# Which PSUM pool a level's product of the gated linear attention takes its bank from

## The chip, the cores and the metric

The kernel runs on one core of a Trainium2 chip. A core has five engines that run side by side, each with its own queue in order: TensorE (PE, matrix products; PEld is its loading of weights), VectorE (DVE), ScalarE (ACT), GpSimd (POOL) and SyncE (SP, which here only issues transfers). PE writes its products to PSUM, which this kernel uses as eight banks of 128 x 512 float32. DVE and ACT read them from there. The metric is the device time of one execution in microseconds (us). Lower is better.

## The reference

One layer of a hybrid decoder over 16 meta tokens and 2048 real tokens of width 1024. A normalised input u goes through one wide projection. Its columns feed two branches: a Mamba-2 state space scan (SSD, 16 heads in 4 groups, chunks of 128) and a gated linear attention (GLA, 4 heads, chunks of 64 in the reference). Both are normalised, projected, weighted by sigmoid gates, summed, projected again and added to the input. The part that the change touches is the attention within a chunk:

```python
rel = gi[:, :, :, None, :] - gi[:, :, None, :, :]
rel = jnp.exp(jnp.where(causal, rel, -jnp.inf))
att = jnp.einsum('bhtk,bhsk,bhtsk->bhts', qi, ki, rel)
o_intra = jnp.einsum('bhts,bhsv->bhtv', att, vi)
```

`gi` is the running sum of the log decay, so that each pair (t, s) has a decay of its own for every one of the 128 key channels.

## The kernel before, in words

The work has two phases. The first takes the 2048 tokens in four blocks of 512. Per block it projects u for four SSD groups and then for four GLA heads (`ssd_proj`, `gla_proj`), and beside these projections it runs the scans (`ssd_scan`, `gla_scan`). The products of the projections are float32 made of three products of rounded halves (`accum`, L188 to L190). The second phase makes the gates, the two branch projections and the output projection by a product scheme of seven products in place of eight (`Stage`).

**Order.** The scans are Python generators. After each part of a projection, `step()` takes every running scan one `yield` further, the oldest first, so that a scan's few products stand on PE between long runs of projection products. In the first phase the order of PE and of SP is the one written by hand. In the second only SP's is. The rest (DVE, ACT, POOL, and PE in the second phase) is put in order by a planner at build time, which has a model of the times.

**GLA scan.** For one head and one block of 512 tokens, `gla_scan` does not form the decay of each pair. It builds the triangle of a chunk in seven levels, with blocks of 1, 2, 4, 8, 16, 32 and 64 rows. `pack` (ACT, L706) gathers the operand of a level, `level` makes two 128 x 128 products per level on PE (L712, float32, which the profile shows as two records each), then takes over the part that belongs to the level: for the first level a copy on ACT (L717), for the others a predicated copy on DVE (L720). DVE then multiplies keys and queries by the decay of that level (L725), and `pack` gathers for the next. There are 16 such scans with 7 levels, 112 in all, mostly one level per step. After the levels, `diag` (L757), the transposes of keys and of the scores (L769, L774), four chunk products `po` with the running state (L782 to L791), and transposes of the output (L801, read by L802) follow.

**PSUM.** Three pools share the eight banks: `pj` (3) for the projections, `pt` (3) for transposes and small products, `pc` (2) for the scans' products. A tile gets a bank when a bank of its pool has been read for the last time, and the first product into it waits for that. The users in the first phase are:

- `pc`: in `ssd_scan` the scores (L529), and per chunk `py` (L572, L573, read by L580 and L583) and `pst` (L575, read by L578). In `gla_scan` the four `po` (read by L787, L789 and L791), in block 0 the meta products (L524, L743), and before the change the levels.
- `pt`: in `ssd_scan` a chunk's three transposes (L548, read by L551, L553, L554 and L557) and the two output transposes (L607, read by L609). In `gla_scan` the meta keys of block 0 (L735, read by L737), `diag`, L769, L774 and L801. Elsewhere the row factors of u (L281), the small products of `dt_chain` (L400 to L418) and of `gates`. Two tiles are held for long: one of the four of the first projection of a block (`zm`, L461), and in block 0 a head's meta values (`pv5`, L634, read by L638).

Of the kernel before, what the change touches and what calls it, by code (L numbers as in the profile page):

```python
# [40 lines left out]
def trunk_kernel(ctx: ExitStack, tc: tile.TileContext, xm, xmt, w_feat, w_tok, w_zm, w_br, w_o,  # L41
# [7 lines left out]
    def mk(pool, shape, dt, tag, **kw):  # L49
        cnt[0] += 1  # L50
        return pool.tile(shape, dt, tag=tag, name=f"{tag}_{cnt[0]}", **kw)
# [72 lines left out]
    pt = ctx.enter_context(tc.tile_pool(name="pt", bufs=3, space=bass.MemoryType.PSUM))  # L124
    pc = ctx.enter_context(tc.tile_pool(name="pc", bufs=2, space=bass.MemoryType.PSUM))

    def bank(pool, tag):
        return mk(pool, [P, 512], F32, tag)
# [534 lines left out]
    def gla_scan(o, h, kq, vals, gs):  # L663
# [5 lines left out]
        def odd_even(half, start, nb, skip):  # L669
            pitch = list(kq.ap[0])  # L670
            return bass.AP(kq.tensor, kq[:, 0, start:].offset, [pitch, [2 * half, nb], [skip, 2], [1, half]])
# [31 lines left out]
        def pack(half):  # L703
            packed[0] = mk(wk, [P, 2 * P], F32, "c1", bufs=NC1)
            nb = P // half
            nc.scalar.activation(packed[0].rearrange("p (b two h) -> p b two h", two=2, h=half),  # L706
                                 odd_even(half, m0, nb, k_to_q + 2 * P + half), AF.Copy)

        def level(half):
            ps = bank(pc, "pc")  # L710
            for r in range(2):
                nc.tensor.matmul(ps[:, r * P:(r + 1) * P], packed[0][:, r * P:(r + 1) * P],  # L712
                                 odd_even(half, m0 + (r + 2) * P, P // (2 * half), k_to_q - 2 * P + half),
                                 start=True, stop=True)
            pv2 = ps[:, :256].rearrange("p (r t) -> p r t", t=P)
            if half == 1:
                nc.scalar.activation(xa, pv2, AF.Copy)  # L717
            else:
                mi = msk[:, LEVELS.index(half)].unsqueeze(1).to_broadcast([P, 2, P])
                nc.vector.copy_predicated(xa, mi, pv2)  # L720
            nb = BLK // (2 * half)
            kv = odd_even(half, m0, nb, k_to_q + half)
            at = place[half][0]
            other = bass.AP(ex.tensor, ex[:, at + 1:].offset, [list(ex.ap[0]), [2, nb], [-1, 2], [0, half]])
            nc.vector.tensor_tensor(kv, kv, other, op=ALU.mult)  # L725
            if half < P // 2:
                pack(2 * half)

        pack(1)
        yield  # L730
        level(1)
        yield
        if m0:
            ps = bank(pt, "pt")
            nc.tensor.transpose(ps[:META, :P], km, ident)  # L735
            btm = mk(wk, [P, P], F32, "bt")
            nc.scalar.activation(btm[:META], ps[:META, :P], AF.Copy)  # L737
        level(2)
        yield
        level(4)  # L740
        yield
        if m0:
            ps = bank(pc, "pc")  # L743
# [23 lines left out]
        ps = bank(pt, "pt")  # L767
# [4 lines left out]
        ps = bank(pt, "pt")  # L772
# [25 lines left out]
        for j in range(2):  # L798
            ps = bank(pt, "pt")
# [238 lines left out]
    for st in stages:  # L1038
        begins.append(len(order))
        for n in range(0, st.npairs, 2):  # L1040
            ps = PS if (st, n) != (stages[-1], st.npairs - 2) else PS[:5] + (4, 3)
# [176 lines left out]
```

## Time and profile before

| what | value |
|---|---|
| time, median of 3 runs | 2353.59 us (2347.39 to 2354.49) |
| the profiled execution's own time | 2356.76 us |
| its span in the trace | 2355.0 us |
| PE busy | 2261.0 us, 96% of the span |
| PEld busy | 1963.7 us, 83% |
| DVE busy | 1450.1 us, 62% |
| ACT busy | 1143.9 us, 49% |
| POOL busy | 678.5 us, 29% |
| granted TensorE clock, mean | 0.986 |

The span runs from the first to the last instruction, and the own time is that of the whole execution. Busy is the time in which an engine ran an instruction. An engine's idle time is put down to the instruction that released it. The ends of products are modelled in the trace, so that short idle times of PE are less sure than long ones. The first phase ends at about 1565 us of the span.

### The profile page before, as it was taken

The page shows a single profiled execution, that of the slowest core. Times are in us where ns is not written, and L with a number is a line of the kernel's source. Part 1 is how long each engine was busy: PE and PEld are TensorE (multiplying, and loading weights), DVE is VectorE, ACT ScalarE, POOL GpSimd, SP SyncE. Part 2 cuts the span into 40 slices and gives each one's busy share as a digit, 9 for nine tenths or more (in the row PEclk, how much of TensorE's full clock was granted, in tenths as well). Part 3 has the DMA queues.
Part 4 walks back from the last instruction along what each step waited for, and adds up shares of the span by engine and source line. Part 5 has one row for each costly group of instructions (what it writes and reads, how often), then busy time and mean ns, then how long its engine had stood idle before and what let it go on. Part 6 is the DMA issues. An engine that isn't in the chain of part 4 may idle for free. (4 is left out here: it accounts for less than half of the span.)

```text
span 2355.0 us, 35946 instructions
## 1 busy us (share of the span) xinstructions
PE 2261.0 (96%) x12673; PEld 1963.7 (83%) x12673; DVE 1450.1 (62%) x2547; ACT 1143.9 (49%) x2582; POOL 678.5 (29%) x681
## 2 busy tenths in 40 slices
PE   7999999999899999999999999979999999999998
PEld 6889888898788988888888888868888888888876
DVE  5666655466554466655447654455578964779776
ACT  5656544365533265633346443354545454554443
POOL 4344333122211122221112200027433355323331
PEclk9999999999999999999999999989999999999999
DMA  8666765668676676766577644457677876688743
GB/s 305 228 207 225 254 226 200 215 206 252 213 242 201 210 223 216 255 213 222 173 226 245 209 143 165 134 168 249 209 246 264 292 235 214 225 284 272 257 155 123
DMA packets 301540, 518.01 MB, mean 220 GB/s; under 512 B 27696, under 2 KB 143664, under 8 KB 301360
## 3 DMA queue, kind: packets, MB, share of 16 engines
q1 hardware_dynamic: 200400, 402.84, 52.6%
q10 hardware_dynamic: 100960, 112.88, 13.8%
q8 instruction: 99, 1.62, 0.3%
q14 instruction: 81, 0.66, 0.1%
HBM read 368.42 MB, written 147.19 MB: 219 GB/s over the span
## 5 line engine op out<-in xcount | busy, mean ns | idle before, releaser
L188 PE MATMUL pj<-u,whl 128*128 128x512 f32 (+1 forms) x1184 | 448.7, 379 | 14.4 <-ACT acc L481 7.7
L190 PE MATMUL pj<-u,whl 128*128 128x512 f32 (+1 forms) x1184 | 432.9, 366 | 1.4 <-DVE dw L391 0.8
L189 PE MATMUL pj<-u,whl 128*128 128x512 f32 (+1 forms) x1184 | 432.2, 365 | 0.0
L188 PE MATMUL pj<-whl,u 128*128 128x256 f32 (+1 forms) x992 | 291.5, 294 | 2.2 <-ACT u L306 1.5
L190 PE MATMUL pj<-whl,u 128*128 128x256 f32 (+1 forms) x992 | 283.9, 286 | 1.4 <-DVE u L308 1.4
L189 PE MATMUL pj<-whl,u 128*128 128x256 f32 (+1 forms) x992 | 283.8, 286 | 0.9 <-POOL whl L169 0.9
L188 PEld LDWEIGHTS pj<-u,whl 128*128 128x128 f32 x1184 | 226.8, 192 | 52.1 <-ACT acc L481 9.3
L188 PE MATMUL pj<-b,a 128*128 128x512 f32 x640 | 252.9, 395 | 6.0 <-ACT sn L930 3.6
L190 PEld LDWEIGHTS pj<-u,whl 128*128 128x128 f32 x1184 | 226.2, 191 | 37.6 <-POOL whl L169 1.8
L189 PEld LDWEIGHTS pj<-u,whl 128*128 128x128 f32 x1184 | 226.7, 191 | 32.2
L189 PE MATMUL pj<-b,a 128*128 128x512 f32 x640 | 250.7, 392 | 1.8 <-DVE b L889 1.8
L190 PE MATMUL pj<-b,a 128*128 128x512 f32 x640 | 251.8, 393 | 0.0
L188 PEld LDWEIGHTS pj<-whl,u 128*128 128x128 f32 x992 | 191.6, 193 | 3.8 <-ACT u L306 2.0
L190 PEld LDWEIGHTS pj<-whl,u 128*128 128x128 f32 x992 | 191.2, 193 | 2.1 <-DVE u L308 2.1
L189 PEld LDWEIGHTS pj<-whl,u 128*128 128x128 f32 x992 | 191.6, 193 | 1.5 <-POOL whl L169 1.1
L80 POOL TENSOR_TENSOR wr<-wr 128x256 f32<-128x256 f32 x80 | 65.8, 823 | 433.7 <-DMA wr<-y 146.9
L169 POOL TENSOR_TENSOR whl<-wr,whl 128x512 fp32r<-128x512 f32 (+1 forms) x100 | 132.0, 1326 | 192.8 <-ACT whl L168 167.6
L889 DVE TENSOR_TENSOR b<-br,b 128x512 fp32r<-128x512 f32 x196 | 153.8, 805 | 45.9 <-ACT b L888 41.9
L904 POOL TENSOR_TENSOR as<-ar,ar 128x512 f32<-128x512 f32 x40 | 59.2, 1481 | 403.9 <-DMA ar<-in_w_br 151.7
L485 DVE SCALAR_TENSOR_TENSOR acc<-cin,hcw,acc 128x512 f32<-128x512 f32 (+1 forms) x192 | 155.7, 811 | 31.4 <-ACT acc L481 29.8
L888 ACT ACTIVATE b<-br 128x512 fp32r<-128x512 f32 x196 | 119.5, 626 | 99.9 <-DMA br<-br_t 36.4
L914 DVE TENSOR_TENSOR a<-ar,a 128x512 fp32r<-128x512 f32 x160 | 128.6, 812 | 59.2 <-ACT a L913 58.5
(270 smaller groups left out, 4903.5 us busy)
## 6 DMA issues: line engine op xcount, KB each, us to landing
whl<-k_s SPq DMA_DIRECT2D x96, 512.0 KB, 4.6
whl<-k_g SPq DMA_DIRECT2D x96, 512.0 KB, 4.0
whl<-k_v SPq DMA_DIRECT2D x48, 512.0 KB, 3.6
whl<-k_z SPq DMA_DIRECT2D x36, 512.0 KB, 3.8
wr<-in_w_feat SPq DMA_DIRECT2D x64, 256.0 KB, 4.3
k_s<-whl SPq DMA_DIRECT2D x32, 512.0 KB, 3.7
cb<-cumd ACTq DMA_DIRECT2D x64, 256.0 KB, 6.0
y<-gg ACTq DMA_DIRECT2D x64, 256.0 KB, 5.0
```

The lines of the kernel that those rows point to most:

```text
L80: nc.gpsimd.tensor_tensor(o, x, y, op=ALU.subtract)
L169: nc.gpsimd.tensor_tensor(hl[:, 1], raw, hl[:, 0].bitcast(F32), op=ALU.subtract)
L188: nc.tensor.matmul(ps, sh, mh, start=first, stop=False, **kw)
L189: nc.tensor.matmul(ps, sh, ml, start=False, stop=False, **kw)
L190: nc.tensor.matmul(ps, sl, mh, start=False, stop=last, **kw)
L485: nc.vector.scalar_tensor_tensor(acc, cin[:, k:k + tt], hcw[:, ti, k:k + 1], acc, op0=ALU.mult, op1=ALU.add)
L888: nc.scalar.activation(t[:, 0], raw, AF.Copy)
L889: nc.vector.tensor_tensor(t[:, 1], raw, t[:, 0].bitcast(F32), op=ALU.subtract)
L904: nc.gpsimd.tensor_tensor(s1, a21, a22, op=ALU.add)
L914: nc.vector.tensor_tensor(t[:, 1], src, t[:, 0].bitcast(F32), op=ALU.subtract)
```

## The change

In `level` the tile of a level's product is taken from `pt` in place of `pc`. The sizes of the pools stay, and so do the products, what reads them, and the order on PE in the first phase and on SP.

```diff
         def level(half):
-            ps = bank(pc, "pc")
+            ps = bank(pt, "pt")
             for r in range(2):
                 nc.tensor.matmul(ps[:, r * P:(r + 1) * P], packed[0][:, r * P:(r + 1) * P],
                                  odd_even(half, m0 + (r + 2) * P, P // (2 * half), k_to_q - 2 * P + half),
```

## The prediction

> **What bounds the kernel now.** First the page: busy time by engine and the slices.
>
> ```profile
> span 2355.0 us, 35946 instructions
> ...
> PE 2261.0 (96%) x12673; PEld 1963.7 (83%) x12673; DVE 1450.1 (62%) x2547; ACT 1143.9 (49%) x2582; POOL 678.5 (29%) x681
> ...
> PE   7999999999899999999999999979999999999998
> ```
>
> PE is busy in nearly every slice and no other engine is above 62%, so the time is PE's work plus the idle time that is left on PE. A change that moves no product can only act through that idle time. Next, the first phase from the first level on, in the table by stretches (PE busy stands first after the length):
>
> ```profile
> 240.00:1565.00 1325.00, 1277.09 (x7745) 1129.53 (x7744) 737.64 (x1480) 608.47 (x1503) 273.13 (x341) 0.99 0.65 209
> ```
>
> 1325.0 - 1277.1 = 47.9 us of PE's idle time lie where the levels run. Third, the view of line L712, the level's product: what ended PE's idle time before it (us, times), and then the same for its loading of weights, PEld.
>
> ```profile
>   DVE s_ssd L578: 12.3, 7
>   DVE c L583: 5.2, 5
>   ACT c L706: 5.0, 1
>   DVE s_gla L745: 1.6, 3
> ```
>
> ```profile
> L712 PEldq EVENT_SEMAPHORE  x63: 51/51/51, 253.6 to 1519.1; - x63
> ...
>   issue: 13.6, 10
>   ACT junk L791: 10.1, 21
>   ACT acc L262: 6.6, 2
>   ACT c L706: 5.2, 1
>   DVE s_gla L745: 2.8, 3
>   ACT bt L557: 1.4, 1
>   ACT cin L478: 1.2, 1
>   ACT sq L560: 0.9, 1
> ```
>
> L578, L583, L745 and L791 do not make the level's operand. They read `pst`, `py`, the meta product and `po`, the other users of `pc`. Only L706 is the operand. So nearly all of this is waiting for a bank: a step that issues two tiles of `pc` and then a level asks for three banks of a pool of two. The timeline shows both kinds. First the longest wait, beside an SSD scan:
>
> ```profile
> 628.65 0.59 PE L575 MATMUL pc<-c,bt 128*128 128x256 f32 x2
> 633.27 1.20 PE L712 MATMUL pc<-act,c 128*128 128x128 f32 x4 [4.03 <-DVE s_ssd L578]
> ```
>
> ```profile
> 632.62 0.16 DVE L263 TENSOR_TENSOR ss<-ss 128x1 f32<-128x1 f32 x1 [2.40 <-ACT acc L262]
> 632.70 0.42 DVE L578 TENSOR_TENSOR s_ssd<-s_ssd,pc 128x256 f32<-128x256 f32 x1
> ```
>
> L578, which frees the bank, stands on DVE behind L263, which waits for a square on ACT. The projections stand behind the level on PE. Then the short kind, beside a GLA scan that issues `po`:
>
> ```profile
> 319.02 0.70 PE L786 MATMUL pc<-s_gla,act 128*128 128x256 f32 x2
> 319.28 0.38 ACT L791 ACTIVATE junk<-pc 128x256 bf16<-128x256 f32 x1
> 319.54 0.20 ACT L791 ACTIVATION_READ_ACCUMULATOR junk<-pc 128x1 f32 x1
> ...
> 319.80 0.52 PEld L712 LDWEIGHTS pc<-act,c 128*128 128x128 f32 x4 [0.48 <-ACT junk L791]
> ```
>
> PE itself looks busy here, because the modelled end of L786 covers the gap; PEld shows it.
>
> **The change, part by part.** *Waits that go.* By PE's rows, without L706: 12.3 + 5.2 + 1.6 = 19.1 us in 15 waits. By PEld's rows, without L706: 13.6 + 10.1 + 6.6 + 2.8 + 1.4 + 1.2 + 0.9 = 36.6 us in 39 waits. PE's rows leave out the 21 short waits, and PEld's count time in which the product before still ran. The true price lies between, and I take the middle, 28 us. It is the largest term.
>
> Does something else wait in the same place? The operand has been there for long: at 633.27 `pack` had ended at 627.06 (the row of L706 that started at 626.53):
>
> ```profile
> 626.53 0.53 ACT L706 ACTIVATE c<-act 128x256 f32<-128x256 f32 x1
> ```
>
> The level could follow L575 at once, and the next SSD tiles of `pc` come a whole step later, when their banks have been read. So I let the saved time stand in full. PE is in order, so each saved wait moves all that follows on it; SP's order is fixed and its transfers into the weight buffers wait for PE's last reading, so they move with it.
>
> *Waits that come.* `pt` has three banks, and a level now waits for the reader of an older tile of `pt`. Counting through the hand-written order step by step, most steps ask for at most three tiles of `pt`, and the third finds a bank that was read a step ago. These do not.
>
> Heads of block 0: the step issues L769, L774 and L735 while `pv5` has held a bank, and then a level. The first bank to come free is that of L735, read by L737.
>
> ```profile
> 409.17 0.64 PE L712 MATMUL pc<-act,c 128*128 128x128 f32 x4
> ...
> 410.14 0.25 ACT L737 ACTIVATE bt<-pt 16x128 f32<-16x128 f32 x1
> ```
>
> L737 ends at 410.39, and the level started at 409.17: 1.2 us, at three heads 3.7 us. Starts of blocks 1 to 3: `zm` holds a bank, L801 takes two, and the level waits for the first reading of L801.
>
> ```profile
> 813.89 0.75 DVE L802 SCALAR_TENSOR_TENSOR gg<-pt,hgw,gg 128x512 f32<-128x512 f32 x1 [0.31 <-PE pt L801]
> ...
> 814.13 0.61 PE L712 MATMUL pc<-act,c 128*128 128x128 f32 x4
> ```
>
> 814.64 - 814.13 = 0.5 us, at three places 1.5 us. A level right behind the two tiles of L607 waits for the first L609 of the two:
>
> ```profile
> 243.01 0.91 PE L712 MATMUL pc<-act,c 128*128 128x128 f32 x4
> ...
> 243.12 1.23 ACT L609 ACTIVATE gg<-pt,hsw 128x512 f32<-128x512 f32 x2
> ```
>
> 243.12 + 1.23/2 = 243.7, 0.7 us, at two places in block 0 that have a third tile held: 1.4 us. The sum is 6.6 us; a few places where the wait is a tenth or two come on top, and I take 8 us. Behind the waiting level stand the projections on PE, and nobody else waits. The lower bound is half, 4 us, if the planner brings the readers forward; the upper is double, 16 us, if DVE and ACT, now fed earlier by PE, reach these readers later than before.
>
> *What the planner moves.* In the built program PE's order in the first phase and SP's are unchanged. On DVE, L720 and L725 come up to five places earlier, almost all in block 0, and L578, L585 and L304 up to four places later; ACT and POOL change by a few neighbours. The state that L578 makes is used a step later, so I set this at nothing; without that cover it would cost the 0.42 us of L578 a time, with four chunks under 2 us. PE has 32 more separate waits in its queue (206 for 174). At the 51 ns of the row above they cost at most 32 x 0.051 = 1.6 us, at least nothing where PE's queue runs ahead. I take 1 us.
>
> *The clock.* In the table by stretches the granted clock is the last value but two.
>
> ```profile
> 631.79:638.62 6.83, 5.35 (x25) 5.38 (x26) 3.34 (x8) 4.32 (x13) 0.77 (x2) 0.50 0.49 187
> 1000.43:1010.67 10.24, 8.67 (x35) 7.80 (x36) 6.53 (x14) 5.53 (x16) 4.49 (x6) 0.50 0.54 188
> ```
>
> ```profile
> 996.80:1000.40 3.60, 1.67 (x15) 1.43 (x13) 0.93 (x2) 3.60 (x12) 1.27 (x2) 1.00 0.99 349
> ...
> 1003.80:1007.20 3.40, 1.86 (x8) 1.44 (x7) 1.53 (x7) 1.62 (x6) 1.28 (x2) 0.50 0.95 363
> ```
>
> Half the clock follows a stretch of about 3.4 us with PE half idle (1.67 of 3.60 us busy), and it lasts while PE stays half idle (1.86 of 3.40). After the wait of 4.03 us it takes 5.35 us of work at half speed; without that wait it goes, 5.35/2 = 2.7 us. Around 1003.80 the level's wait made the stretch half idle; without it the clock should come back a stretch of 3.4 us earlier, 1.7 us. Together 4 us, between 0 and 6, since it hangs on where the stretches fall. The Trainium skill (TensorE: Matmul & The Clock Gate, section The HAM clock gate) has the clock fall after a whole idle window of about 3.4 us; by that only the wait of 4.03 us would count, and the term would be 2.7 us. The rows of 996.80 speak against it: the clock fell after a stretch that was 46% busy.
>
> *The second phase* does not use the levels; a single product group of PE trades places early in it. It moves forward as a block.
>
> The sum: -28 + 8 + 1 - 4 = -23 us. The profiled execution had 2356.8 us itself and would have 2333.8. The median of the runs shown is 3.2 us lower, and the same change takes it to 2353.6 - 23 = 2330.6, rounded 2331 us.
>
> **The rivals.** *Part is given back.* The evacuations on DVE and ACT are late in many steps, and `pt` waits for them just as `pc` did. With the upper bound of 16 us for new waits and no gain in the clock the change is -28 + 16 + 1 = -11 us: 2343 us. For it: L720 and L737 stand in busy queues. Against it: the counted places are few.
>
> *No change.* If the saved time turns up at once in the next wait on PE (the operand of another scan, the weights), the time stays 2354 us, as it would if the level's tile found no free bank more often in three than in two. Against it: at 633.27 the operand had been there for 6.2 us. The Trainium skill (TensorE: Matmul & The Clock Gate, section HAM oscillation) reports a kernel where double-buffering PSUM gave no further gain; the rows of L712 show that here banks do hold PE up.
>
> *Slower.* `pt` becomes the bound. It has more users than `pc`, and where one bank is held by `pv5` or `zm` the levels share two banks with the transposes. If each of the 28 levels of block 0 waited as at 409.17, 1.2 + 0.15 for the signal, that is 38 us against 28 saved: +10 us, 2364 us. It decides once the new waits pass 28 + 4 - 1 = 31 us, some 23 levels at 1.35 us; counting finds three of that size.
>
> **How the numbers follow.** A difference below 0.3%, 7 us, cannot be told from none here; the three runs shown span 7.1 us. The forecast has 0.72, given back 0.10, no change 0.07, slower 0.11. The first two lie beyond 7 us below, so faster has 0.82. The terms' ends give -36.6 + 4 - 6 = -38.6 and -19.1 + 16 + 1.6 = -1.5; both extremes at once are unlikely, so the range is 2318 to 2350. It takes in the forecast and the gain partly given back, and leaves out the slower case and no change.
>
> **What would show it right or wrong.** Right: L712 waits for L578, L583, L745 and L791 no more; its idle rows sum to some 8 us beside L706, with L737, L802 and L609 named; PE's idle time from 240 us to the phase's end falls from 48 to about 30 us; no half clock near 630 us. The given-back part would show as longer waits of `pt` products (L735, L757, L548) for DVE or ACT, the slower case as L712 waiting for L720 or L737 in many steps. If L712's waits go and PE's idle time stays, the step that failed is that the saved time stands in full.

## The result, and the profile after

The changed kernel took 2341.8 us (median of four, 2340.1 to 2342.8) beside 2353.8 us for the kernel before (2347.4 to 2354.5). The ratio is 0.9954, 95% interval 0.9936 to 0.9973: about 12 us less, where 23 were forecast. A second comparison on another occasion, below, gave 0.9925 (0.9897 to 0.9953), about 17 us. The time lies inside the range; the gain is half to three quarters of the forecast. The profiled execution of the change took 2341.92 us itself.

First the page of the change: span, busy time by engine, and PE's slices.

```profile
span 2340.1 us, 35968 instructions
...
PE 2253.9 (96%) x12673; PEld 1963.0 (84%) x12673; DVE 1451.4 (62%) x2547; ACT 1142.6 (49%) x2582; POOL 673.0 (29%) x681
...
PE   7999999999999999999999999979999999999998
```

The slice in the first phase that showed 8 (the one around 630 us) now shows 9; the 7 that is left near 1550 us is the tail of the last scan and the start of the second phase. Next, the first phase in the table by stretches, up to 10 us earlier than the stretch shown of before (the phase ends 18 us earlier).

```profile
240.00:1555.00 1315.00, 1279.44 (x7788) 1137.36 (x7786) 741.58 (x1485) 613.69 (x1513) 280.56 (x348) 0.99 0.66 212
```

1315.00 - 1279.44 = 35.6 us idle, where 47.9 were and about 30 were forecast. Third, the waits of PE and of its loading of weights at the level's product L712 (us, times, longest).

```profile
PE pt L712 <- ACT c L706: 4.6, 1, 4.6
PE pt L712 <- ACT bt L737: 3.4, 3, 1.1
PE pt L712 <- DVE gg L802: 1.5, 3, 0.5
PE pt L712 <- ACT gg L609: 1.2, 2, 0.8
PE pt L712 <- DVE c L720: 0.3, 2, 0.2
```

```profile
PEld pt L712 <- ACT c L706: 4.7, 1, 4.7
PEld pt L712 <- ACT bt L737: 4.0, 3, 1.3
PEld pt L712 <- issue: 3.7, 8, 0.7
PEld pt L712 <- ACT gg L609: 1.8, 2, 1.2
PEld pt L712 <- ACT whl L168: 1.2, 2, 0.6
PEld pt L712 <- DVE c L720: 0.4, 1, 0.4
```

L578, L583, L745 and L791 are gone from both lists. Beside the operand L706 stand the three readers of `pt` that the prediction named, L737, L802 and L609, and twice L720, with 3.4 + 1.5 + 1.2 + 0.3 = 6.4 us on PE. At the line itself the change did what was forecast. Now the waits on PE that grew, in the same view; the kernel before first, then the change.

```profile
PE pc L786 <- DVE s_gla L787: 6.7, 4, 2.6
...
PE pj L188 <- ACT sn L930: 3.6, 5, 1.8
...
PE pc L572 <- DVE sq L563: 3.2, 2, 2.0
```

```profile
PE pc L786 <- DVE s_gla L787: 11.6, 9, 2.9
PE pj L188 <- ACT sn L930: 7.3, 6, 3.8
PE pc L572 <- DVE sq L563: 5.0, 3, 2.8
```

L786, the product with the running state, waits for the state (L787) of the chunk before it; L930 is an evacuation of the second phase. These are single profiles; further ones of the same two kernels, below, show how far such rows scatter. The timeline of the change shows one such wait in block 1, on DVE and then on PE.

```profile
692.01 0.75 DVE L304 SCALAR_TENSOR_TENSOR acc<-acc,pv,cin 128x512 f32<-128x512 f32 x1 [0.92 <-DMA acc<-in_xmt]
693.46 0.69 DVE L308 TENSOR_TENSOR u<-acc,u 128x512 fp32r<-128x512 f32 x1 [0.70 <-ACT u L306]
694.07 0.68 DVE L650 SCALAR_TENSOR_TENSOR gg<-gg,pj 128x512 f32<-128x512 f32 x1
694.67 0.48 DVE L787 SCALAR_TENSOR_TENSOR s_gla<-s_gla,egl,pc 128x256 f32<-128x256 f32 x1
```

```profile
695.20 0.70 PE L786 MATMUL pc<-s_gla,act 128*128 128x256 f32 x2 [1.78 <-DVE s_gla L787]
```

The same product before:

```profile
701.05 0.70 PE L786 MATMUL pc<-s_gla,act 128*128 128x256 f32 x2 [0.82 <-DVE s_gla L787]
```

The product starts 5.9 us earlier, after a wait of 1.78 in place of 0.82 us. L787 stands on DVE behind L304, which in the change waits 0.92 us for the transfer of `in_xmt`, and before did not: PE came earlier by more than this transfer. This is one place, read from the timeline.

### The profile page after: what moved, and what is told of

It reads as the page before. It is cut to its first block, busy times and chain, and to the rows that moved or that the text cites. A ratio compares the mean times of both kernels' runs of the same rounds, so it can differ in the third digit from the quotient of the medians.

```text
span 2340.1 us, 35968 instructions
## 1 busy us (share of the span) xinstructions
PE 2253.9 (96%) x12673; PEld 1963.0 (84%) x12673; DVE 1451.4 (62%) x2547; ACT 1142.6 (49%) x2582; POOL 673.0 (29%) x681
## 3 DMA queue, kind: packets, MB, share of 16 engines
q8 instruction: 100, 1.64, 0.3%
## 5 line engine op out<-in xcount | busy, mean ns | idle before, releaser
L190 PE MATMUL pj<-u,whl 128*128 128x512 f32 (+1 forms) x1184 | 431.6, 365 | 1.7 <-POOL whl L169 0.9
L190 PE MATMUL pj<-whl,u 128*128 128x256 f32 (+1 forms) x992 | 282.8, 285 | 1.6 <-DVE u L308 1.6
L190 PEld LDWEIGHTS pj<-u,whl 128*128 128x128 f32 x1184 | 224.7, 190 | 37.9 <-POOL whl L169 2.1
L190 PE MATMUL pj<-b,a 128*128 128x512 f32 x640 | 251.8, 394 | 0.0
L190 PEld LDWEIGHTS pj<-whl,u 128*128 128x128 f32 x992 | 190.0, 192 | 2.3 <-DVE u L308 2.3
```

Source lines behind the costliest of these rows:

```text
L190: nc.tensor.matmul(ps, sl, mh, start=False, stop=last, **kw)
```

## The experiments

The baseline shared by the first four runs was 2355.4 us (2348.6 to 2364.9), by the next four 2355.5 us (2350.2 to 2362.4), by the third four 2356.7 us (2350.1 to 2363.5). Ratios are to these, with 95% intervals. The pool is chosen in one line throughout.

**The two kernels again (before_again, after_again).** No edit.

> The kernel before once more, unchanged, for a second profile. What is open is why the first phase of the changed kernel is 18.8 us shorter (the gate stage's first product starts at 1542.4 us against 1561.2) and the whole is only 12 us shorter in the medians. Theory 1 (chance): the second phase is near the limit of its loads and varies from one execution to the next, so the stretch from the gate stage's first product (1561.2) to its last (2342.6), 781.4 us here, changes by 2 us or more in this second profile. Theory 2 (the change itself makes the second phase longer): it repeats to about 1 us, 781 us, and the changed kernel's repeats at 785. Time by both: 2354 us within 0.3%.

> The changed kernel once more, unchanged. Start of the gate stage's first product: 1542 us by both theories. The stretch from there to its last product was 785.4 us (1542.4 to 2327.8). Theory 1 (chance): it falls anywhere between 780 and 786. Theory 2 (the change lengthens the second phase): 785 within 1 us. Time by both 2342 us within 0.2%.

Measured: 2356.2 us, 0.9998 (0.9984 to 1.0012), and 2338.6 us, 0.9925 (0.9897 to 0.9953). The change is worth 12 to 17 us by the two comparisons together, not 23. The second phases were 783.9 and 789.1 us long: the first moved by 2.5 us with no edit at all, and the second lies outside what either theory said, so this pair decided nothing.

**The change in blocks 1 to 3 alone (pt_late), and in block 0 alone (pt_first).**

```diff
-            ps = bank(pc, "pc")
+            ps = bank(*((pt, "pt") if o.b else (pc, "pc")))        # pt_late
+            ps = bank(*((pt, "pt") if not o.b else (pc, "pc")))    # pt_first
```

> Levels take a bank of pt in blocks 1 to 3 only, and of pc in block 0. Theory (the places of the waits): over block 0 (243 to 470 us) the changed kernel fell back by 3.6 us against the one before, since its new waits for L737, L802 and L609 and a longer wait of L786 outweigh what it saved there. Without them the gate stage's first product starts 3 to 4 us earlier than in the changed kernel, at about 1539 us, and the time is about 2338 us. Rival (what is saved anywhere is given back later, at the next wait that does not hang on PE): 2342 us as with the whole change.

> Levels take a bank of pt in block 0 only, and of pc in blocks 1 to 3. Theory (the places of the waits): the gate stage's first product starts about 3.6 us later than in the kernel before, at 1565 us, and the time is 2357 us, slower by 0.15%. Rival (a third bank always pays): not slower than 2354 us, the first product at 1561 or before.

Measured: pt_late 2330.3 us, 0.9893 (0.9877 to 0.9910), 25 us less than before, where the theory had 17 and its rival 13; pt_first 2357.6 us, 1.0016 (1.0003 to 1.0028). In block 0 the change costs more than it brings. Left out there, it is worth a little more than was forecast for the whole. The time of pt_first is the one that was expected, but its profile does not show the late start of the second phase that was to go with it: 1556.4 us, not 1565.

**By heads (pt_head0, pt_heads, pt_new).** The levels of head 0 stand on PE beside an SSD scan, those of heads 1 to 3 beside the `po` products of the GLA scan ahead of them.

```diff
-            ps = bank(pc, "pc")
+            ps = bank(*((pt, "pt") if h == 0 else (pc, "pc")))           # pt_head0
+            ps = bank(*((pt, "pt") if o.b and h else (pc, "pc")))        # pt_heads
+            ps = bank(*((pt, "pt") if h and not o.b else (pc, "pc")))    # pt_new
```

> Levels of head 0 of each block take pt, those of heads 1 to 3 take pc as before. Head 0's levels stand beside the SSD scans of the block (the longer waits, for L578 and L583), heads 1 to 3 stand beside the po chunks of the GLA scan before them (the short waits for L791, which PE's own rows hardly show). From the rows of before, head 0 has 18.0 us of the waits of PE and 23.3 us of those of its weight loading, and about 2.7 us of new waits come. Theory 1 (the short waits beside po are real, but only part of their row: about 0.33 us each, 21 of them, 7 us): 2356 - 18 + 3 - 3 of the clock = 2338, about as the full change, L712 keeping some 20 rows of PEld for junk L791. Theory 2 (the rows of weight loading are the true price for all): 2356 - 23 + 3 - 3 = 2333. Rival (the gain of the full change comes mostly from heads 1 to 3): not over 6 us faster, 2350.

> Levels take pt only in heads 1 to 3 of blocks 1 to 3, where nearly all waits are the short ones beside po. In two profiles of before, line L712 loses about 1.4 us at heads 1 to 3 of block 1, 3.0 of block 2 and, with the block's end, about as much of block 3 (against the shortest time that any profile so far has between the same two products), and the new waits at the block starts take 1.5 us back. Theory 1 (a short wait is worth 0.33 us and is partly given back at L786): 1 to 5 us less than before. Theory 2 (the rows of weight loading are their price, 7 us and more): 7 to 10 us less. Rival (all of it is given back): no change.

> Levels take pt only in heads 1 to 3 of block 0, where the full change has its new waits (L737 at three heads) and few old ones to lose. Theory 1 (this part of the change is a loss of what L712 gains in waits there, 3.8 us, and of later waits at L786): 4 to 7 us more than before. Rival (the new waits replace others, so that they cost nothing): within 2 us of before.

Measured: pt_head0 2333.0 us, 0.9912 (0.9893 to 0.9931); pt_heads 2359.6 us, 1.0009 (1.0000 to 1.0018); pt_new 2361.3 us, 1.0025 (1.0012 to 1.0037). The three are the parts of the change without overlap: 0.0088 of 2356 us is 21 us less, 0.0009 is 2 us more, 0.0025 is 6 us more, together 13 us less. Taken alone, the long waits beside the SSD scans bring all the gain; the 2333 us is theory 2's number, and theory 1's 18 us less lies inside the interval too. The new waits of block 0 cost what theory 1 said. Taken alone, the short waits beside `po` bring nothing, where both theories had a gain: the rival of pt_heads stands. They did go, though; its waits:

```profile
PE pc L712 <- DVE s_ssd L578: 15.5, 7, 6.3
PE pc L786 <- DVE s_gla L787: 10.6, 7, 2.2
```

```profile
PEld pc L712 <- ACT junk L791: 1.4, 3, 0.5
```

L791 is down from the 10.1 us in 21 places of before to 1.4 in 3, and L786 is up from 6.7 to 10.6 us (a further profile of before has 10.2). In pt_head0, whose heads 1 to 3 keep their levels in `pc`, the short waits stay and the long ones are gone:

```profile
PE pc L786 <- DVE s_gla L787: 10.0, 7, 2.5
...
PE pc L712 <- ACT c L706: 4.4, 1, 4.4
...
PE pc L712 <- DVE s_gla L745: 1.6, 3, 0.5
PE pt L712 <- ACT gg L609: 1.2, 2, 0.7
```

```profile
PEld pc L712 <- ACT junk L791: 10.0, 21, 0.5
```

The parts do not simply add. The other division of the change, pt_late and pt_first, comes to 25 - 4 = 21 us less, not 13, and the two sums differ by a little more than their intervals allow together (about 8 us). In pt_late the short waits of blocks 1 to 3 are gone too, and L786 has not grown beyond the values of before (its wait first, then L791 in the view of L712):

```profile
PE pc L786 <- DVE s_gla L787: 8.1, 6, 1.9
```

```profile
  ACT junk L791: 1.5, 3
```

By the ratios pt_late is 4 us faster than pt_head0, though their intervals overlap. So that the short waits are worth nothing is shown for pt_heads, and pt_late does not bear it out.

**Pools chosen place by place (pt_chosen).** `pt` where the rows show a wait to go, `pc` where the change adds one.

```diff
-            ps = bank(pc, "pc")
+            ps = bank(*((pt, "pt") if (h == 0 and 1 < half < 64 if not o.b else (h, half) != (3, 32)) else (pc, "pc")))
```

> Levels take pt wherever the rows show a wait to go, and pc at the places where the full change waits for a reader of pt: in block 0 all of heads 1 to 3 and the first two levels and the last of head 0 take pc, in blocks 1 to 3 the level of 32 rows of head 3. From the rows of before, 19.4 us of PE's waits and 31.5 us of those of its weight loading go, and about 0.5 us of new waits come. Theory 1 (what the waits come to is gained less what L786 and the second phase give back, some 10 us): at or a little under the kernel with pt in blocks 1 to 3, 2326 to 2330. Rival (beyond about 20 us every further wait saved turns up in the next one): no better than that kernel, 2330 to 2336.

Measured: 2331.7 us, 0.9903 (0.9887 to 0.9919). This is within the rival's bounds, at their lower end: no better than pt_late, though it has more waits to lose and fewer new ones (the two intervals overlap).

**The state product earlier (after_state, before_state).**

```diff
             accum(po[:, 256:], [t[:, c] for t in kdt], vc, True, True)
-            accum(po[:, :256], [t[:, c] for t in atp], vc, True, False)
-            nc.tensor.matmul(po[:, :256], q[:, c * P:(c + 1) * P], s_gla[:, h], start=False, stop=True)
+            if c % 2:
+                accum(po[:, :256], [t[:, c] for t in atp], vc, True, False)
+            nc.tensor.matmul(po[:, :256], q[:, c * P:(c + 1) * P], s_gla[:, h], start=c % 2 == 0, stop=c % 2 == 1)
+            if c % 2 == 0:
+                accum(po[:, :256], [t[:, c] for t in atp], vc, False, True)
```

> The change, and of each pair of chunks the first one's product with the running state (L786, here L787) goes ahead of its three products with the scores. L787 (here L788) of that chunk can start about 0.65 us earlier, while the second chunk's state product keeps its place. The second one waits in the profile of after for s_gla in 9 places with 11.6 us. Theory 1 (part of the saved waits is given back there, because PE now comes earlier than the state): at 0.65 us a place some 5 to 6 us less than the changed kernel on the same chip, and the row of that wait under 7 us. Theory 2 (the row only shows scatter, and the missing gain lies elsewhere): within 2 us of the changed kernel.

> The kernel before with the same reordering of the state product, and the levels in pc. The profile of before has 6.7 us in 4 places on that wait. Theory 1 (the wait grows through the change): at 0.65 us a place 2 to 3 us less than the kernel before, so that the reordering is worth about twice as much in the changed kernel. Theory 2 (scatter): the reordering is worth the same in both.

Measured: after_state 2339.3 us, 0.9932 (0.9918 to 0.9945), before_state 2357.8 us, 1.0009 (0.9995 to 1.0023). Theory 1 missed in both, and theory 2's numbers came out, but the edit did not do what both took for granted. The waits of DVE in after_state, where the update of the state is L790, show why.

```profile
DVE s_gla L790 <- PE pc L787: 19.0, 24, 0.8
DVE s_gla L790 <- PE pc L190: 9.8, 4, 4.6
```

The reordered chunk ends with the scores' L190, and the update, which reads only the other half of the bank, now waits for that: the last product of the bank releases it in either order, so the update could not start earlier. The Trainium skill (PSUM — Partial Sum Buffer, section PSUM bank collisions raise a hardware error) says to guard PSUM between two engines by bank and quadrant of partitions, or simply by bank, and not by address; that fits these rows. So this pair does not tell the two theories apart.

**More PE work ahead of the second phase (after_hold, before_hold).** 48 repeated products, which compute nothing new.

```diff
-        for i in range(2):
-            nc.tensor.matmul(diag, ones_r, pdt[i], start=i == 0, stop=i == 1)
+        for i in range(50 if (o.b, h) == (3, 3) else 2):
+            nc.tensor.matmul(diag, ones_r, pdt[i % 2], start=i % 2 == 0, stop=i % 2 == 1)
```

> The change, with the two products of the diagonal (L757) of the last GLA scan repeated 24 times more: 48 products of about 0.4 us, 19 us of PE just ahead of the second phase, which compute nothing new. The other engines and the transfers get that time to run ahead. Theory 1 (the second phase is longer with the change because PE reaches it earlier than the transfers and ACT do): its length falls from 785 to 789 us back to about 782, and the kernel takes about 15 us more than the changed one. Theory 2 (another order by the planner, or scatter): the length stays at 785 to 789, and the kernel takes 19 us more.

> The kernel before with the same 48 repeated products ahead of the second phase. Both theories: the second phase is 780 to 784 us long, and the kernel takes 18 to 19 us more than before. If its length falls by several us, waits at the start of the second phase are there without the change too.

Measured: after_hold 2348.5 us, 0.9955 (0.9938 to 0.9972), before_hold 2360.4 us, 1.0020 (1.0006 to 1.0034). The price was misjudged by both theories. The products took 14.26 us for 50 (timeline of after_hold), so 13.7 us for the 48, and cost about 5 us in the kernel before (1.4 to 8 by the interval) and about 7 in the change (the difference of 0.9955 and 0.9925, each known to 4 to 7 us; beside the 0.9954 of the result it is nothing).

```profile
1518.98 14.26 PE L757 MATMUL pt<-sq,ones_r 128*128 128x512 f32 x50
```

The second phase, from the first to the last of its products, was 783.0 us long in before_hold and 782.2 in after_hold. That is theory 1's length, but the work was planned anew around the 48 products, and the time did not follow. It settles nothing alone.

**Two further profiles of each (before_b, before_c, after_b, after_c).** No edit.

> The kernel before, a further profile. Theory 1 (the change lengthens the second phase and L786's waits): second phase not over 784 us from its first to its last product, and about 5 us of lost starts at L786. Theory 2 (scatter between executions): the same spread as the changed kernels, 781 to 789 us and 5 to 11 us.

> The change, a further profile. Theory 1: second phase 785 us or more, and about 10 us of lost starts at L786. Theory 2 (scatter): as often under 784 us as over, L786 anywhere between 5 and 11 us.

> As the other further profile of the kernel before: not over 784 us and about 5 us by theory 1, 781 to 789 us and 5 to 11 us by theory 2.

> As the other further profile of the change: 785 us or more and about 10 us by theory 1, no different from the kernel before by theory 2.

Measured, with the two earlier profiles of each kernel, in us:

| | before | again | b | c | mean | change | again | b | c | mean |
|---|---|---|---|---|---|---|---|---|---|---|
| own time | 2356.8 | 2352.3 | 2354.9 | 2359.4 | 2355.8 | 2341.9 | 2345.3 | 2335.4 | 2340.2 | 2340.7 |
| second phase starts | 1561.2 | 1554.3 | 1557.2 | 1562.6 | 1558.8 | 1542.4 | 1542.1 | 1536.9 | 1542.8 | 1541.1 |
| its length | 781.4 | 783.9 | 783.5 | 782.7 | 782.9 | 785.4 | 789.1 | 784.4 | 783.3 | 785.6 |
| PE at L786 for L787 | 6.7 | 7.1 | 6.8 | 10.2 | 7.7 | 11.6 | 12.0 | 9.7 | 11.9 | 11.3 |

The rows of the second phase's products, before and after, from which starts and lengths come (first and last start at the end):

```profile
L188 PE MATMUL pj<-b,a x640: 387/394/628, 1561.2 to 2342.6; 128*128 128x512 f32 x160
```

```profile
L188 PE MATMUL pj<-b,a x640: 387/394/632, 1542.4 to 2327.8; 128*128 128x512 f32 x160
```

L786 waits 3.6 us more in the mean with the change; the single values nearly separate (10.2 before against 9.7 after). The second phase is 2.7 us longer in the mean, and there the values overlap (783.9 before against 783.3 after). One profile of each kernel could not have shown either.

## Why the forecast was half wrong

I set the starts of the same products side by side in the profiles with the same order of PE, and summed at each line by how much a start came later than the shortest time that any profile has from the product ahead. By this count L712 loses 33 to 34 us in each of the four profiles of before and 11 to 12 in those of the change: 22 us net.

- *Waits that go, -28, and waits that come, +8.* Right: level by level, in the mean of the four profiles, about 31 us go and 9 come, which is 22 net for the 20 forecast; 7 of the 9 lie in block 0. That L737, L802 and L609 make them, and mostly in block 0, was right too.
- *"I let the saved time stand in full."* This is the step that failed, and the forecast's own test named it (PE's idle time fell by 12 us, not by 18). Its reason was read off the longest wait, beside an SSD scan, and then held for all. Of the 22 us at L712, 17.8 are left at the start of the second phase and 15.1 in the time. Cut at the first level of head 0 and of head 1 in each block, the first phase shows where, against the mean of before. The three stretches with head 0 of blocks 1 to 3 are together 20.5 to 21.6 us shorter in the four profiles of the change, and L712 loses 19 us less there: the long waits are kept in full, as pt_head0 (21 us) agrees. The stretches with heads 1 to 3 of these blocks are 1.2 us shorter to 0.8 longer, though L712 loses 4 us less there: the short waits are not kept. Block 0 is 1.7 to 4.2 us longer, though L712 loses only 0.7 more there. (The profiles of before scatter by up to 2.4 us around their mean in these sums.) That L786's wait grew is shown by the table; that it grew because PE came ahead of the update on DVE is read from the timeline, and no run took that wait away. In the single profiles of pt_heads and pt_late the stretches with heads 1 to 3 did get shorter, by 5.9 and 7.9 us, so what decides whether the short waits are kept stays open.
- *"It moves forward as a block."* The phase starts 17.8 us earlier in the mean and ends 15.1 earlier. The 2.7 us between are within what single profiles scatter, so whether the change costs them stays open. Over the sixteen profiles without repeated products the phase is 786.4 us long in the mean where it starts before 1545 us and 783.9 where it starts after 1550, which leans to a cost.
- *The clock, -4.* Right where it was looked for, and smaller in sum. At the two places that the prediction named, near 631 and 1003 us, the clock records have half the clock for 11.9 us in the mean of the four profiles of before and 6.0 in those of the change, which is 3.0 us of work at half speed. In the pair of the result the stretch of 6.83 us near 631 us is gone; two of the other three profiles of the change still have 3.4 us of it there. In the tail of the last scan the change has 14.5 us of it against 11.1, which is 1.7 back. Over the phase it is 27.3 against 29.9 us, 1.3 us of work.
- *Separate waits, +1.* Too small to be seen.

The sum of the means: -22 at L712, +4 in the rest of the first phase (the wait at L786 grows by 3.6 in the table, and the clock is in it), +2.7 in the second phase, which is -15 where the own times differ by 15.1. So the rival "part is given back" described the outcome better, and by another way than it said: not by longer waits for `pt`, which came out as forecast, but behind the line. That its 2343 us lies so near the 2341.8 measured is luck. The rival "no change" was right for heads 1 to 3 of blocks 1 to 3 taken alone (1.0009). The rival "slower" was right for block 0 (1.0016, and 1.0025 for its heads 1 to 3), and the wait for L737, which its reason foretold, is in the rows; that the bank held by `pv5` is the cause is read from the program, and no run freed that bank.

## What to carry to other kernels

A wait taken from an engine in order is worth its length only as long as the engine does not then wait for the next thing instead. Here waits of up to 4 us between long runs of other work were kept whole, and eighteen of up to 0.5 us beside a recurrent state were not, in the full change. Price the two kinds apart, and do not count the short ones until a run shows them. When a tile is moved to another pool, move it only in the places where that pool has a bank to spare: the same edit in three blocks of four was worth 25 us, in all four 12 to 17.

## What the runs showed of the hardware

Extra PE work in a stretch where PE waits was partly paid back, by the clock and by waits that ended meanwhile. In the change PE goes from L757 to the second phase with waits between, and its granted clock is half for most of it (stretches of 3.40 us; PE's busy time, then the clock, then DMA).

```profile
1528.10:1531.50 3.40, 1.64 (x11) 1.00 0.83 254
1531.50:1534.90 3.40, 2.53 (x9) 0.51 0.94 304
1534.90:1538.30 3.40, 2.61 (x9) 0.50 0.55 204
1538.30:1541.70 3.40, 3.10 (x12) 0.50 0.39 119
```

The whole way from L757 on, and then the same way behind the 48 products, which ran at the full clock in 8.5 us (all engines, PE first):

```profile
1526.10:1542.40 16.30, 12.59 (x50) 9.49 (x49) 11.70 (x22) 9.05 (x23) 0.00 (x0) 0.62 0.60 194
```

```profile
1533.24:1541.73 8.49, 7.21 (x46) 5.56 (x45) 5.29 (x11) 3.16 (x11) 0.00 (x0) 1.00 0.17 64
```

From the start of L757 to the second phase the change takes 16.4 us (1525.96 by its timeline to 1542.4) and after_hold 22.7: 6.3 us more for 13.7 us of products. Of the 7.4 us paid back, 2.4 are idle time of PE (16.30 - 12.59 = 3.7 us against 8.49 - 7.21 = 1.3), and the rest, 5 us, goes with the clock. The clock fell after a stretch with 1.64 of 3.40 us busy, as at 996.80 in the prediction, and stayed at half through two stretches with 2.53 and 2.61 busy. The Trainium skill (TensorE: Matmul & The Clock Gate, section The HAM clock gate) has it fall after an idle window and rise after one of sustained work. The rows agree with the second (the clock came back after the stretch with 3.10 busy) and not with the first: it was lost at 48% busy.
